# Input loads in equal halves, small loads moved, a value tile copied in place, recurrent states first on VectorE

## The chip, the cores and the metric

The kernel runs on one core of a Trainium2 chip. The metric is the time of one execution on the device in microseconds (us); the median of several runs is compared. The core has five engines that run side by side, each working through its own instructions in order: TensorE (PE in the profile; its weight loads are PEld), VectorE (DVE), ScalarE (ACT), GpSimd (POOL) and SyncE (SP), which here only issues DMA transfers. [...]

## The reference

One layer of a diffusion backbone on 640 tokens: 128 context tokens and 512 latent tokens, each a row of 1024 numbers. All in 32-bit floats.

```
shift, scale, gate = split(silu(c) @ w_ada + b_ada)
h    = rmsnorm(x, g_pre) * (1 + scale) + shift
proj = h @ w_in                                  # 3840 columns
a    = attention: 8 heads of 64; latent tokens see a window of the grid plus 256 cached context keys
r    = two gated linear recurrences (forward, backward), 4 heads, state 64 x 64 a head
f    = real part of a 2-D Fourier transform over positions and channels, then a 256 x 256 matrix
out  = concat(a * silu(ga), rmsnorm(r) * silu(gr), f * silu(gf)) @ w_out
y    = x + gate * rmsnorm(out, g_post)
```

Context and latent tokens have modulation vectors of their own. The latent recurrences start from given states; the context's final states, keys and values are outputs too.

## The kernel before

All products of weights with activations are done three times on TensorE, since each 32-bit operand is split into a high and a low part (hi, lo: a cast on ScalarE, line 130, and a subtraction on VectorE, line 131), and hi x hi, hi x lo and lo x hi are added up in PSUM. `mm` at line 113 issues every product, `tr` at line 127 every transpose through TensorE.

Start: `load_x` (line 217) reads the input in five tiles of 128 tokens. Each tile comes in two transfers, columns 0 to 639 into `xa` and 640 to 1023 into `xb`. `scale_x` sums the squares of `xa` on ScalarE (line 225) and of `xb` on VectorE (line 226), makes the reciprocal root and scales both halves on VectorE (lines 230, 231). `start_stream` then takes eight modulation steps k: two 512 KB blocks of the modulation weights (wss) are multiplied with the activated conditioning vector (`mod_cols`), the result is brought into columns, the scaled input's column block k is transposed (`xcols` picks it) and modulated into hT. The weights of the first three steps are loaded ahead. `zf_stream` multiplies the first projection blocks as the blocks of hT appear.

Small constants come first: cc (the conditioning vectors) and lbl (the logits of the recurrences' lower bound) on SP's queue, bss, gpre and sel on GpSimd's. sel is a 0/1 selector for the gate vectors; `gate_vectors` (line 853) copies it at line 855 and uses it late in the kernel. cc is needed for csil (line 171), lbl for a short chain on VectorE and ScalarE (lines 154 to 160).

Loads of weights go through `load_raw`, which chains each SP transfer behind the weight transfer issued before it (`wdma`, an order of issue, not a wait); `load` queues other transfers behind the last weight transfer so far.

The rest: a fixed list (FILL) says in which order projection blocks are traced: zb0, qr0, zb1, qr1, ir0 for the recurrences, then four pairs of attention heads P0 to P3 between gate and Fourier blocks. Generators for the two recurrences (`recurrence(p)`, two heads each), the attention and the gate vectors are woven in by a small planner (`Order`) with assumed latencies. The framework then orders the traced instructions of every engine: by its own model of their durations it takes the ready one of the highest priority, which is the order of tracing unless `tc.high_priority()` lifts a block of them. So an edit in one place can change the order elsewhere.

A recurrence runs seven levels over blocks of 1, 2, 4 ... 64 tokens: copies of the operands on ScalarE (lines 468 to 471), four multiplications on VectorE (474 to 477), products on TensorE and a masked copy into AL and AC on VectorE (458). Then come the states: for each of two directions four 128 x 128 products into a PSUM tile pst, the context's final state copied out (`fin`, line 519), and along the chunks state = state x decay + product (line 532, three chunks times two heads). The decays lie in small tiles of tag "m" (four buffers, shared with softmax scratch); pst and the level products share five PSUM buffers of tag "b".

For each pair of attention heads, `by_token` (line 345) transposes the value tile, five blocks, into PSUM; the fifth is copied by ScalarE into an "m" tile (line 354), and ScalarE and VectorE split the result into vs. Tiles of tag "t", the value tile among them, share 18 buffers.

Of the kernel before, what the change touches and what calls it, by code (L numbers as in the profile page):

```python
# [12 lines left out]
ACT = mybir.ActivationFunctionType  # L13
ALU = mybir.AluOpType
# [3 lines left out]
P = 128  # L18
D = 1024
KT = 8  # L20
NT = 640
# [50 lines left out]
def mixer_kernel(ctx: ExitStack, tc: tile.TileContext, A, O):  # L72
    nc = tc.nc
    sc, ve, gp, te, sy = nc.scalar, nc.vector, nc.gpsimd, nc.tensor, nc.sync
# [12 lines left out]
    def nm(s):  # L87
        n_[0] += 1
        return f"{s}_{n_[0]}"

    def T(cols=NT, dt=F32, tag=""):
        return tp.tile([P, NT], dt, tag="t", name=nm("t" + tag))[:, :cols]

    def PE_():
        return tp.tile([P, 512], F32, tag="pe", name=nm("pe"), bufs=WB["pe"])

    def S(cols):
        if cols <= 16:
            return sp.tile([P, 16], F32, tag="s", name=nm("s"))[:, :cols]
        return sp.tile([P, 320], F32, tag="m", name=nm("m"), bufs=WB["m"])[:, :cols]  # L100
# [4 lines left out]
    def PB(tag="b"):  # L105
        return ps.tile([P, 512], F32, tag=tag, name=nm("pb"), bufs=WB["p" + tag])
# [3 lines left out]
    def mm(out, lhsT, rhs, start=True, stop=True):  # L110
        n, m = rhs.free_size(), lhsT.free_size()
        od.now += 1e-3 * (n * 0.4167 * 4 if rhs.dtype == F32 else max(n * 0.4167, m * 0.83)) + 2e-3
        return te.matmul(out, lhsT, rhs, start=start, stop=stop).ins  # L113
# [11 lines left out]
    def tr(out, src):  # L125
        od.now += 0.107
        last_tr[0] = te.transpose(out, src, ident).ins  # L127

    def split(src, hi, lo, hi_eng=None, lo_eng=None):
        (sc.copy if hi_eng is None else hi_eng.tensor_copy)(hi, src)  # L130
        (ve if lo_eng is None else lo_eng).tensor_sub(lo, src, hi.bitcast(F32))  # L131
# [5 lines left out]
    def const(name, shape, dt=F32, dma=gp.dma_start):  # L137
        t = cp.tile([P, *shape], dt, tag=name, name=name)
        if name in A:
            dma(t, A[name])  # L140
        return t

    cc = const("cc", [KT, 2], dma=sy.dma_start)
    lbl = const("lbl", [2, 2], dma=sy.dma_start)
    bss = const("bss", [KT, 2])
    gpre = const("gpre", [KT])
    sel = const("sel", [2, P])
    RS = [slice(0, 64), slice(64, 128)]
    eps = cp.tile([P, 1], F32, tag="eps", name="eps")
    ve.memset(eps, EPS)  # L150
# [11 lines left out]
    def rsqrt_mean(ss, n):  # L162

        sc.activation(ss, ss, ACT.Sqrt, bias=eps, scale=1.0 / n)
        ve.reciprocal(ss, ss)
# [7 lines left out]
    wdma, nb = [], [1]  # L173

    def load_raw(src, tag, shape=(KT, P)):
        t = (tp if tag == "vs" else wp).tile([P, *shape], F32, tag=tag, name=nm(tag), bufs=WB[tag])
        with tc.issue_after(wdma[-1]) if wdma else ExitStack():
            wdma.append(sy.dma_start(t, src).ins)
        return t
# [10 lines left out]
    def load(t, src):  # L190

        with tc.issue_after(wdma[-1]) if wdma else ExitStack():
            sy.dma_start(t, src)

    def mod_cols(out, w, chain):

        t = od.now
        for k in range(KT):
            run_mm(chain, out[32 * (k % 4):32 * (k % 4) + 32, :], csil[:, k, :], w[:, k, :], start=(k < 4), stop=(k >= 4))
        od.now = t + 0.45  # L200

    shift, G, rstd = const("shift", [KT, 2]), const("G", [KT, 2]), const("rstd", [5])
    hT = [big.tile([P, KT, NT], F32R, tag=f"hT{j}", name=f"hT{j}") for j in range(2)]
    xa, xb = [T(tag="xa") for _ in range(5)], [T(384, tag="xb") for _ in range(5)]

    def xcols(i, k):
        return (xa[i] if k < 5 else xb[i])[:, k % 5 * P:k % 5 * P + P]
    zf_w, zf_acc = [], [[PB("f"), PB("f")], [PB("f"), PB()]]

    def mm3(out, w, k, u, first, last):  # L210
# [5 lines left out]

    def load_x():
        for i in range(5):
            load(xa[i], A["x"][i * P:(i + 1) * P, 0:NT])
            load(xb[i], A["x"][i * P:(i + 1) * P, NT:D])  # L220

    def scale_x():
        for i in range(5):
            ss2 = S(2)
            sc.activation(T(), xa[i], ACT.Square, accum_out=ss2[:, 0:1])
            ve.tensor_tensor_reduce(PE_()[:, 0:384], xb[i], xb[i], 1.0, 0.0, op0=ALU.mult, op1=ALU.add,
                                    accum_out=ss2[:, 1:2])
            ve.tensor_add(rstd[:, i:i + 1], ss2[:, 0:1], ss2[:, 1:2])
            rsqrt_mean(rstd[:, i:i + 1], D)
            ve.tensor_scalar(xa[i], xa[i], rstd[:, i:i + 1], 0.0, op0=ALU.mult, op1=ALU.add)  # L230
            ve.tensor_scalar(xb[i], xb[i], rstd[:, i:i + 1], 0.0, op0=ALU.mult, op1=ALU.add)
# [11 lines left out]

    def start_stream():
        load_x()
        raws, zraw = [], []

# [98 lines left out]
    def by_token(src, copy_last=False):  # L346

        pt = PB(), PB("f")
        for i in range(5):
            tr(pt[i // 4][:, i % 4 * P:i % 4 * P + P], src[:, i * P:(i + 1) * P])  # L350
        last = pt[1][:, 0:P]
        if copy_last:
            last = S(P)
            sc.copy(last, pt[1][:, 0:P])
        return [(slice(4 * j, 4 + j), (pt[0], last)[j].rearrange("p (i e) -> p i e", e=P)) for j in range(2)]

# [66 lines left out]
    def recurrence(p):  # L423
# [88 lines left out]
        for d in range(2):  # L512
            Td = (Tf, Tb)[d]
            pst = PB()
            for a, i in enumerate([0] + order[d][:3]):
                mm(pst[:, a * P:(a + 1) * P], kt[d][:, a * P:(a + 1) * P], vr[p][:, i, :])
            fin = sp.tile([P, 64], F32, tag="fin", name=nm("fin"), bufs=2)
            for hh in range(2):
                ve.tensor_copy(fin[RS[hh], :], pst[RS[hh], 64 * hh:64 * hh + 64])
            sy.dma_start(O["o_st"][d, p], fin)  # L520
            sall = T(512)
            gp.memset(sall, 0.0)
            for a, i in enumerate(order[d]):
                for hh in range(2):
                    r = RS[hh]
                    cdst = slice(a * P + 64 * hh, a * P + 64 * hh + 64)
                    if a == 0:
                        gp.tensor_copy(sall[r, cdst], late["st"][r, p, d, :])
                    else:
                        ip = order[d][a - 1]  # L530
                        cs = slice((a - 1) * P + 64 * hh, (a - 1) * P + 64 * hh + 64)
                        ve.scalar_tensor_tensor(sall[r, cdst], sall[r, cs], Td[r, ip:ip + 1], pst[r, cdst],  # L532
                                                op0=ALU.mult, op1=ALU.add)
                Sst[d][i] = sall[:, a * P:(a + 1) * P]
        yield LAT["st"]

# [314 lines left out]
    gg = [[None, None], [None, None]]  # L851

    def gate_vectors():
        selr = cp.tile([P, 2, P], F32R, tag="selr", name="selr")
        gp.tensor_copy(selr, sel)
        for q in range(8):
            yield f"block{WG + q}"
            hf = q // 4
            w = load_raw(A["wg"][q], "raw")
            if q % 4 == 0:  # L860
                gbias = T(512), T(512)
                for t, name in zip(gbias, ("bgate", "gpost")):
                    load(t, A[name][hf * 512:hf * 512 + 512].partition_broadcast(P))
                if True:
                    if q == 0:
                        gc = sp.tile([P, 2, 512], F32, tag="masks", name="gc", bufs=1)
                    gg[0][hf], gg[1][hf] = gc[:, hf, :], T(512)
                else:
                    gg[0][hf], gg[1][hf] = T(512), T(512)
            if q % 2 == 0:  # L870
                rows = [sp.tile([P, 256], F32R, tag="AC", name=nm("row"), bufs=2) for _ in range(2)]
            pm, es = PB("f"), slice(q % 2 * P, q % 2 * P + P)
            mod_cols(pm[:, 0:P], w, [])
            split(pm[:, 0:P], *[t[:, es] for t in rows])
            if q % 2 == 0:
                continue
            yield 1.0
            pg, cs = PB("f"), slice(q % 4 * P - P, q % 4 * P + P)
            for d in range(2):
                for a in range(2):  # L880
                    mm(pg[:, d * 256:d * 256 + 256], selr[:, d, :], rows[a], start=(a == 0), stop=(a == 1))
            for d in range(2):
                g = gg[d][hf][:, cs]
                ve.tensor_add(g, pg[:, d * 256:d * 256 + 256], gbias[0][:, cs])
                ve.tensor_mul(g, g, gbias[1][:, cs])
# [108 lines left out]

    od.add(late_consts())
    od.add(recurrence(0))
    od.add(recurrence(1))
    od.add(attentions())
    od.add(gate_vectors())
    od.add(fill())  # L1000
    od.run()
# [136 lines left out]
```

## Time and profile before

| | |
|---|---|
| median of 3 runs | 434.32 us (433.76 to 434.38) |
| the profiled execution | 434.13 us |
| its span | 432.3 us |
| TensorE busy | 409.4 us (95%) |
| VectorE busy | 303.0 us (70%) |
| ScalarE busy | 205.8 us (48%) |
| GpSimd busy | 7.4 us (2%) |
| moved by DMA | 47.62 MB, 110 GB/s over the span |

A line of the profile names the start and length in us (or a count, busy time and mean), the engine, the line of the kernel, the operation, output<-input, and the number of instructions as x16. In brackets stands how long the engine had been idle before it and what released it. SPq and POOLq are queues that issue transfers.

### The profile page before, as it was taken

The numbers are of one execution on the slowest core, as the hardware profiler recorded it, in microseconds if no ns is written. First come the engines' busy times: TensorE is split into PE (matmuls) and PEld (weight loads), VectorE is DVE, ScalarE is ACT, GpSimd is POOL, SyncE is SP. The second block draws the span as 40 slices with busy tenths as digits, with TensorE's granted clock in tenths as the row PEclk, the third lists the DMA queues.
The fourth block names the chain that finished last, engine by engine and source line by source line (L and its number), as shares of the span: only waits on it lengthen the run. The fifth ranks groups of instructions, "written<-read, shape, count | busy, mean of one in ns | idle before, by whom it ended". The sixth has DMA issues, their size and how long they took to land.

```text
span 432.3 us, 8308 instructions
## 1 busy us (share of the span) xinstructions
PE 409.4 (95%) x3176; PEld 372.6 (86%) x3176; DVE 303.0 (70%) x866; ACT 205.8 (48%) x551; POOL 7.4 (2%) x23
## 2 busy tenths in 40 slices
PE   0699999999998999999999999999999999999994
PEld 0488999999988998999899989899898889988884
DVE  3775579999896966885598657786679748471164
ACT  6525466566342526754445634744466553341331
POOL 2000000000020000000000000000000000000000
PEclk9999999999999999999999999999999999999998
DMA  7996154101202021122012522245323202245032
GB/s 236 414 407 237 49 176 141 61 16 50 99 12 75 9 62 49 56 98 74 33 60 72 143 73 90 90 154 159 105 101 122 89 9 102 85 156 198 0 147 99
DMA packets 19528, 47.62 MB, mean 110 GB/s; under 512 B 3184, under 2 KB 6912, under 8 KB 19488
## 3 DMA queue, kind: packets, MB, share of 16 engines
q1 hardware_dynamic: 19376, 46.94, 31.3%
q8 instruction: 25, 0.41, 0.4%
q0 software_dynamic: 112, 0.14, 0.3%
q14 instruction: 15, 0.12, 0.1%
HBM read 43.80 MB, written 3.28 MB: 109 GB/s over the span
## 4 chain that ended last, share of the span: by engine, by line
PE 90%; DVE 4%; DMA 3%; ACT 1%; issue 0%; SPq 0%; DVEq 0%
PE pb L113 84%; PE pb L127 7%; DMA vs<-wss 1%; DMA txa<-x 1%; DVE t L532 1%; DVE AL L458 1%; DVE AL L495 0%; ACT L688 0%; DVE lo L131 0%; DVE t L960 0%; ACT hi L130 0%; ACT pe L688 0%; ACT pe L689 0%; DVE t L475 0%; DVE t L474 0%
## 5 line engine op out<-in xcount | busy, mean ns | idle before, releaser
L113 PE MATMUL pb<-hT,hi 128*128 128x320 f32 x896 | 207.8, 316 | 0.5 <-DVE t L131 0.4
L113 PEld LDWEIGHTS pb<-hT,hi 128*128 128x128 f32 x896 | 149.5, 188 | 6.4 <-issue 1.1
L113 PE MATMUL pb<-hT,lo 128*128 128x320 f32 x448 | 139.7, 313 | 0.0
L113 PEld LDWEIGHTS pb<-hT,lo 128*128 128x128 f32 x448 | 84.1, 188 | 1.4 <-DVE G L274 0.2
L131 DVE TENSOR_TENSOR lo<-raw,hi 128x1024 fp32r<-128x1024 f32 x35 | 42.7, 1221 | 21.8 <-ACT hi L130 21.5
L130 ACT CAST hi<-raw 128x1024 fp32r<-128x1024 f32 x35 | 36.7, 1049 | 35.2 <-PE pb L113 19.5
L113 PE MATMUL pb<-t,t 64*128 64x128 f32 (+2 forms) x414 | 43.1, 291 | 1.9 <-DVE t L532 1.5
L113 PEld LDWEIGHTS pb<-t,t 64*128 64x128 f32 (+1 forms) x414 | 36.2, 188 | 6.3 <-issue 2.3
L113 PE MATMUL pb<-hi,mh 128*128 128x512 f32 (+1 forms) x108 | 32.1, 376 | 0.0
L130 ACT CAST pT<-pb 128x256 fp32r<-128x256 f32 x64 | 22.9, 371 | 16.3 <-DVE pT L131 9.8
L131 DVE TENSOR_TENSOR pT<-pb,pT 128x256 fp32r<-128x256 f32 x64 | 26.3, 416 | 1.6 <-ACT pT L130 1.3
L113 PEld LDWEIGHTS pb<-hi,mh 128*128 128x128 f32 x108 | 19.4, 189 | 3.2
L113 PE MATMUL pb<-pT,mh 128*128 128x512 f32 (+1 forms) x102 | 22.2, 364 | 0.0
L688 ACT ACTIVATE pe<-pb,s 128x256 f32<-128x256 f32 x32 | 15.2, 476 | 13.0 <-DVE s L687 7.7
L127 PE MATMUL pb<-ident,pe 128*128 128x128 f32 x136 | 20.8, 274 | 0.5 <-ACT pe L689 0.5
L943 ACT ACTIVATE t<-pb 128x512 f32<-128x512 f32 (+1 forms) x11 | 6.0, 551 | 30.5 <-PE pb L113 30.5
L113 PEld LDWEIGHTS pb<-pT,mh 128*128 128x128 f32 x102 | 17.7, 189 | 3.1
L113 PE MATMUL pb<-lo,mh 128*128 128x512 f32 (+1 forms) x54 | 20.2, 373 | 0.0
L127 PEld LDWEIGHTS pb<-ident,pe 128*128 128x128 f32 x136 | 16.5, 140 | 1.7 <-ACT pe L689 0.7
L458 DVE COPY_PREDICATED AL<-masks,pb 128x512 f32<-128x512 uint32 x24 | 16.5, 738 | 1.9 <-PE pb L113 1.8
L113 PE MATMUL pb<-pT,vs 128*128 128x256 f32 (+1 forms) x96 | 17.2, 321 | 0.0
L699 DVE TENSOR_TENSOR o<-pb,o 64x512 f32<-64x512 f32 (+1 forms) x16 | 7.8, 487 | 13.3 <-ACT o L698 13.2
(209 smaller groups left out, 630.1 us busy)
## 6 DMA issues: line engine op xcount, KB each, us to landing
raw<-win SPq DMA_DIRECT2D x30, 512.0 KB, 3.3
pT<-wss SPq DMA_DIRECT2D x12, 512.0 KB, 10.2
raw<-wg SPq DMA_DIRECT2D x8, 512.0 KB, 3.4
raw<-wout SPq DMA_DIRECT2D x8, 512.0 KB, 3.3
t<-x SPq DMA_DIRECT2D x10, 256.0 KB, 5.8
o_y<-t SPq DMA_DIRECT2D x9, 256.0 KB, 2.1
vs<-wss SPq DMA_DIRECT2D x4, 512.0 KB, 9.1
tbl<-tbl SPq DMA_DIRECT2D x4, 512.0 KB, 3.3
```

The lines of the kernel that those rows point to most:

```text
L113: return te.matmul(out, lhsT, rhs, start=start, stop=stop).ins
L127: last_tr[0] = te.transpose(out, src, ident).ins
L130: (sc.copy if hi_eng is None else hi_eng.tensor_copy)(hi, src)
L131: (ve if lo_eng is None else lo_eng).tensor_sub(lo, src, hi.bitcast(F32))
L458: ve.copy_predicated(out, mk.to_broadcast([P, i1 - i0, P]), src)
L532: ve.scalar_tensor_tensor(sall[r, cdst], sall[r, cs], Td[r, ip:ip + 1], pst[r, cdst], op0=ALU.mult, op1=ALU.add)
L688: sc.activation(pe[:, 256:512], ss[:, 256:512], ACT.Exp, bias=m[:, 1:2], accum_out=m[:, 3:4])
L699: ve.tensor_add(out, src[r, :], out)
L943: sc.activation(T(512)[:, cs], po[:, 0:cs.stop - cs.start], ACT.Square, accum_out=ssb[:, j:j + 1])
```

## The change

- `load_x` and `scale_x`: each tile is loaded as 512 + 512 columns; the ten loads enter the chain `wdma` of weight transfers. ScalarE squares 512 columns instead of 640, VectorE 512 instead of 384.
- lbl and cc are loaded through ScalarE's queue, lbl first.
- sel is no longer loaded at the start through GpSimd's queue but in `gate_vectors`, through `load`, on SP's queue.
- `by_token` with `copy_last` copies the fifth block over the fifth block of its source, in place of a tile of its own.
- In `recurrence`, the copies to `fin` and the state updates get high priority.

```diff
-    cc = const("cc", [KT, 2], dma=sy.dma_start)
-    lbl = const("lbl", [2, 2], dma=sy.dma_start)
+    lbl = const("lbl", [2, 2], dma=sc.dma_start)
+    cc = const("cc", [KT, 2], dma=sc.dma_start)
     bss = const("bss", [KT, 2])
     gpre = const("gpre", [KT])
-    sel = const("sel", [2, P])
...
-    xa, xb = [T(tag="xa") for _ in range(5)], [T(384, tag="xb") for _ in range(5)]
+    xa, xb = [T(512, tag="xa") for _ in range(5)], [T(512, tag="xb") for _ in range(5)]
     def xcols(i, k):
-        return (xa[i] if k < 5 else xb[i])[:, k % 5 * P:k % 5 * P + P]
+        return (xa[i] if k < 4 else xb[i])[:, k % 4 * P:k % 4 * P + P]
...
     def load_x():
         for i in range(5):
-            load(xa[i], A["x"][i * P:(i + 1) * P, 0:NT])
-            load(xb[i], A["x"][i * P:(i + 1) * P, NT:D])
+            for u, t in enumerate((xa[i], xb[i])):
+                with tc.issue_after(wdma[-1]) if wdma else ExitStack():
+                    wdma.append(sy.dma_start(t, A["x"][i * P:(i + 1) * P, 512 * u:512 * u + 512]).ins)
     def scale_x():
...
-            sc.activation(T(), xa[i], ACT.Square, accum_out=ss2[:, 0:1])
-            ve.tensor_tensor_reduce(PE_()[:, 0:384], xb[i], xb[i], 1.0, 0.0, op0=ALU.mult, op1=ALU.add,
+            sc.activation(T(512), xa[i], ACT.Square, accum_out=ss2[:, 0:1])
+            ve.tensor_tensor_reduce(PE_(), xb[i], xb[i], 1.0, 0.0, op0=ALU.mult, op1=ALU.add,
                                     accum_out=ss2[:, 1:2])
...
         if copy_last:
-            last = S(P)
+            last = src[:, 4 * P:5 * P]
             sc.copy(last, pt[1][:, 0:P])
...
-            for hh in range(2):
-                ve.tensor_copy(fin[RS[hh], :], pst[RS[hh], 64 * hh:64 * hh + 64])
+            with tc.high_priority():
+                for hh in range(2):
+                    ve.tensor_copy(fin[RS[hh], :], pst[RS[hh], 64 * hh:64 * hh + 64])
...
-                        ve.scalar_tensor_tensor(sall[r, cdst], sall[r, cs], Td[r, ip:ip + 1], pst[r, cdst],
-                                                op0=ALU.mult, op1=ALU.add)
+                        with tc.high_priority():
+                            ve.scalar_tensor_tensor(sall[r, cdst], sall[r, cs], Td[r, ip:ip + 1], pst[r, cdst],
+                                                    op0=ALU.mult, op1=ALU.add)
...
     def gate_vectors():
+        sel = const("sel", [2, P], dma=load)
         selr = cp.tile([P, 2, P], F32R, tag="selr", name="selr")
         gp.tensor_copy(selr, sel)
```

## The prediction

> **What bounds the kernel now.** I read the page first, then who TensorE waited for, then two stretches in order of time.
>
> ```profile
> span 432.3 us, 8308 instructions
> PE 409.4 (95%) x3176; PEld 372.6 (86%) x3176; DVE 303.0 (70%) x866; ACT 205.8 (48%) x551; POOL 7.4 (2%) x23
> ```
>
> ```profile
> PE pb L113 <- DMA vs<-wss: 14.0, 1, 14.0
> PE pb L113 <- DVE t L532: 1.5, 1, 1.5
> PE pb L127 <- ACT pe L689: 0.5, 1, 0.5
> PE pb L113 <- DVE t L131: 0.4, 1, 0.4
> PE pb L113 <- DVE AL L458: 0.4, 1, 0.4
> ```
>
> ```profile
> 0.00:14.00 14.00, 0.04 (x4) 0.07 (x6) 6.52 (x30) 9.25 (x19) 3.08 (x11) 1.00 0.84 278
> 119.00:133.00 14.00, 12.10 (x110) 10.64 (x107) 13.09 (x39) 5.07 (x14) 2.42 (x6) 1.00 0.04 9
> 133.00:160.00 27.00, 27.00 (x225) 26.31 (x225) 20.16 (x53) 10.86 (x29) 1.91 (x6) 1.00 0.19 58
> ```
>
> The page says TensorE bound, 95%. The change touches none of its matmuls, so it can only win where TensorE stands still. The list of waits names all those places: 14.0 us before the first weights of the modulation (wss) land, 1.5 us once for the state instruction L532 of the recurrence, and three waits of half a microsecond or less. In the table of stretches (after the length: busy TensorE, weight loads, VectorE, ScalarE, GpSimd, clock, share of DMA, GB/s) the start is a DMA stage (0.84 busy). From 119 to 133 VectorE is busy 13.09 of 14.00 us and TensorE only 12.10. In the next 27 us TensorE is full, and the list has no long wait after it, so time won in either place should reach the end.
>
> **The start.** What changes: two small loads leave SP's queue, the selector's load (sel) leaves the front, and the input comes as 512 + 512 columns in place of 640 + 384.
>
> ```profile
> 0.73 0.39 SPq L140 DMA_DIRECT2D cc<-cc  x1
> 1.18 0.42 SPq L140 DMA_DIRECT2D lbl<-lbl  x1
> 1.65 0.42 SPq L193 DMA_DIRECT2D txa<-x  x1
> 7.49 0.74 ACT L225 ACTIVATE t<-txa 128x640 f32<-128x640 f32 x1 [1.43 <-DMA txa<-x]
> 9.87 0.56 DVE L226 CUSTOM_DVE_ANT_0 pe<-txb 128x384 f32<-128x384 f32 x1 [1.03 <-DMA txb<-x]
> 14.34 0.55 DVE L230 TENSOR_SCALAR txa<-txa,rstd 128x640 f32<-128x640 f32 x1
> 14.97 0.50 PEld L127 LDWEIGHTS pb<-ident,txa 128*128 128x128 f32 x3 [0.38 <-DVE txa L230]
> ```
>
> ```profile
> 6.00:8.00 2.00, 0.00 (x0) 0.00 (x0) 0.30 (x2) 0.57 (x2) 0.40 (x1) 1.00 1.01 287
> 10.00:12.00 2.00, 0.00 (x0) 0.00 (x0) 1.96 (x10) 1.83 (x6) 0.00 (x0) 1.00 1.07 420
> ```
>
> ```profile
> sel<-sel POOLq DMA_DIRECT2D x1, 128.0 KB, 4.4
> ```
>
> - Queue: SP issues the first input load at 1.65; with cc and lbl gone it can go at 0.73, 0.92 us sooner. The DMA engines are full from then on (share 1.01 and above), so the whole train of input and weights moves by that much.
> - sel: 128 KB out of that train at the 287 GB/s of its stretch is 0.45 us for all that lands behind it. Together the first weights land 0.92 + 0.45 = 1.37 us sooner.
> - VectorE: the sum of squares of the second half grows from 384 to 512 columns. Its own row has one width only, so I take the slope of other two-operand rows of VectorE shown below, 0.83 us for 640 columns and 0.49 for 320: 0.34 / 320 x 128 = 0.14 us a tile. VectorE has waits ahead of the first three tiles (the 1.03 us above is the last of them) and runs without a break afterwards, so three tiles pay: 0.41 us. The two scalings trade 128 columns and their sum stays. TensorE's first transposes wait for exactly this work (0.38 us at 14.97, for L230), so what gets through is not 1.37 but 1.37 - 0.41 = 0.96 us. ScalarE's Square becomes shorter by the same columns.
> - ScalarE issues cc and lbl ahead of its first table load, some 0.8 us by SP's rows. This costs nothing: lbl lands half a microsecond sooner than before, and ScalarE stood idle 1.43 us ahead of the second Square. Were that cover gone, it would cost the 0.8.
> - sel again: SP issues it behind the weights of modulation step 3, one issue and 128 KB, 0.31 us at 420 GB/s, ahead of the weights of steps 4 to 7. Their cover is in these rows:
>
> ```profile
> pT<-wss SPq DMA_DIRECT2D x12, 512.0 KB, 10.2
> 24.04 2.39 SPq L178 DMA_DIRECT2D pT<-wss  x3
> 41.71 1.08 PE L113 MATMUL pb<-pT,csil 128*32 128x128 f32 x32
> ```
>
> The last of them is issued by 26.43, lands some 10.2 us later, at about 36.6, and is used at 41.71: 5 us of cover for 0.31. sel's only reader (selr on GpSimd) is needed far later by the gate vectors.
>
> I take 0.9 us for the start; its bounds are 0 (all given back on VectorE or in issue order) and 1.4.
>
> **The states.** Rows of VectorE, TensorE and ScalarE, then groups of the stretch from 119 to 134:
>
> ```profile
> 125.78 0.48 DVE L477 TENSOR_TENSOR t<-t,m 128x320 f32<-128x320 f32 x1
> 126.38 0.45 DVE L519 COPY fin<-pb 64x64 f32<-64x64 f32 x2
> 127.48 0.49 DVE L474 TENSOR_TENSOR t<-t,m 128x320 f32<-128x320 f32 x1
> 132.11 1.22 DVE L532 SCALAR_TENSOR_TENSOR t<-t,m,pb 64x64 f32<-64x64 f32 x4
> 50.38 0.83 DVE L241 TENSOR_TENSOR hT<-t,hT 128x640 fp32r<-128x640 f32 x1
> ```
>
> ```profile
> 124.63 1.16 PE L113 MATMUL pb<-t,t 128*128 128x128 f32 x8 [0.36 <-DVE AL L458]
> 127.59 0.49 PE L113 MATMUL pb<-t,t 64*128 64x128 f32 x2
> 131.00 0.31 PE L113 MATMUL pb<-hT,lo 128*128 128x320 f32 x1
> 132.84 0.46 PE L113 MATMUL pb<-t,t 64*128 64x128 f32 x2 [1.53 <-DVE t L532]
> 126.29 0.46 ACT L471 COPY t<-t 128x320 f32<-128x320 f32 x1 [0.23 <-DVE t L477]
> 132.79 0.27 ACT L354 COPY m<-pb 128x128 f32<-128x128 f32 x1 [6.03 <-DVE t L532]
> ```
>
> ```profile
> L532 DVE SCALAR_TENSOR_TENSOR t<-t,m,pb 64x64 f32<-64x64 f32 x12 | 3.4, 280 | 0.4
> L519 DVE COPY fin<-pb 64x64 f32<-64x64 f32 x4 | 0.9, 219 | 0.1
> L113 PE MATMUL pb<-hT,hi 128*128 128x320 f32 x20 | 5.0, 329 | 0.0
> L113 PE MATMUL pb<-hT,lo 128*128 128x320 f32 x9 | 2.8, 308 | 0.0
> ```
>
> TensorE's state products of recurrence 0 are issued by 125.8. VectorE then needs 12 + 4 small instructions, 3.4 + 0.9 = 4.3 us, but spreads them from 126.38 to 133.33, since instructions of recurrence 1's levels (L474 at 127.48 is one) stand between. The level products at 132.84 read nothing of the states. They wait because PSUM buffers of tag "b" (five) are still held by the products that L532 reads. With priority the block runs from about 125.8 to 130.1, before TensorE runs dry at 131.31 (131.00 + 0.31), and the 1.53 us go. The instructions pushed aside are late by up to 4.3 us; the 29 projection matmuls of the stretch cover that, if the planner leaves them ahead of the level products.
>
> The copied value tile takes away ScalarE's 6.03 us wait: the tile of tag "m" that L354 wrote was held by the decays which L532 reads. The copy then runs at about 126.8, and the casts of the next weights behind it move up as well. TensorE waited for none of these, so I cost it at nothing; without it the 1.53 us might only have passed to the casts. In exchange the value tile, of tag "t" (18 buffers), lives until its splits have read it. Whoever waits for that buffer is ScalarE or VectorE, and hardly longer than the 6.03 us that the copy itself waited so far, a wait that TensorE's other work covered; I cost it at nothing too.
>
> I take 1.5 us; bounds are the loss worked out below and 1.53 + 0.36 = 1.9.
>
> **The sum.** The profiled run took 434.13 us, 1.8 us around its span of 432.3, and lies 0.19 under the median of 434.32. 434.13 - 0.9 - 1.5 = 431.73, on the median 431.9 us.
>
> **Rivals.**
> 1. The start is given back. TensorE ends its first steps at half its later rate:
>
> ```profile
> 22.57 1.02 PE L113 MATMUL pb<-vs,csil 128*32 128x128 f32 x16
> 26.96 1.08 PE L113 MATMUL pb<-pT,csil 128*32 128x128 f32 x32
> ```
>
> 16 products took 1.02 us at 22.57, and 32 took 1.08 at 26.96. If full rate begins at the same moment although TensorE starts 0.9 us sooner, the time won is filled at half rate and 0.45 remains; the sum is then 434.32 - 0.45 - 1.5 = 432.4. If VectorE or the new order eats all, 432.8. For it: VectorE is full from 9.87 on. Against it: the transposes depend on what moved. [...]
> 2. The wait at 132.84 takes another form. TensorE meets the next unfinished level there and stands about as long; only the start counts, 434.32 - 0.9 = 433.4. For it: VectorE is busy 13.09 of 14 us, and its sum of work is the same. Against it: the wait is for a buffer, not for work.
> 3. Slower: the state block runs over the operands of the next level. L477 at 125.78 feeds ScalarE's copy L471 and that the level products at 127.59. Behind 4.3 us of states L477 starts at 130.1, L471 ends at 131.0, and products placed at 127.59 are 3.4 us late. If TensorE's order leaves them where they are, it pays 3.4 - 1.5 = 1.9 us net, less 0.9 from the start: 435.3. It turns to a loss where fewer than 8 projection matmuls are put in front: 3.4 less the 2.4 of the forecast is 1.0 us, at 27.00 us / 225 = 0.12 us an instruction. The planner orders TensorE with VectorE's delay in view, and 29 such matmuls stand in the stretch, which speaks against it.
> 4. All of it comes through: start 1.4, states 1.9, and a little more where the scratch tile freed in "m" shortens the softmax waits (the 0.5 us for L689): 434.32 - 3.8 = 430.5.
>
> **Chances.** Forecast 0.46, rival 1 0.17, rival 2 0.14, rival 3 0.13, rival 4 0.10. 0.2% is about what a measurement of this kernel can tell, 0.87 us: faster is under 433.45, slower over 435.19. Forecast, rivals 1 and 4 are faster, 0.73; rival 2 lies on the edge, and I give it to "same", with a little of rival 1 for an order of the planner that comes out worse elsewhere: faster 0.71, same 0.16, slower 0.13. The range reaches from rival 4 with a little more, 430.2, over rival 2 to 434.5; above it is rival 3. The forecast's own range is 431.2 to 432.6.
>
> **What would show it.** Right: the first input load at about 0.7 and the first modulation products at about 12.6; transposes some 0.9 us sooner; the 16 state instructions in one block of some 4.5 us; no wait of TensorE for L532; L354 within a microsecond of its transpose. Wrong: a TensorE wait for L458 or L471 near 130; VectorE still scaling when the second modulation product has landed more than a microsecond before; new waits after 160, which would be the planner's order and not a part of the change.

## The result, and the profile after

The changed kernel takes 429.76 us (median of 4 runs, 429.45 to 430.12) beside 434.04 us for the kernel before (4 runs, 433.70 to 434.38): ratio 0.9902, 95% interval 0.9885 to 0.9919. That is 4.28 us less where 2.4 were forecast, and 0.44 us below the range. The profiled execution took 430.12 us beside 434.13.

The line of busy times and the list of TensorE's waits (line, who was waited for, total, times, longest), after the change:

```profile
PE 409.1 (96%) x3176; PEld 372.2 (87%) x3176; DVE 305.0 (71%) x866; ACT 205.3 (48%) x551; POOL 7.0 (2%) x22
```

```profile
PE pb L113 <- DMA vs<-wss: 12.2, 1, 12.2
PE pb L113 <- DVE AL L458: 0.4, 1, 0.4
PE pb L113 <- ACT t L237: 0.3, 1, 0.3
PE pb L127 <- DVE row L266: 0.3, 1, 0.3
```

The wait for the first weights is 1.8 us shorter. Three waits are gone: 1.5 us for the states (L532), 0.5 us for the probabilities (L689) and 0.4 us for L131. Two small ones at the start are new. In the table of stretches TensorE is now full from 133 to 345 (before, it was busy 184.08 of the 185.00 us from 160 on), and from 119 to 133 it gained what the state wait had cost:

```profile
119.00:133.00 14.00, 13.63 (x115) 12.33 (x114) 13.43 (x42) 6.37 (x17) 2.42 (x6) 1.00 0.05 11
133.00:160.00 27.00, 27.00 (x225) 26.20 (x225) 18.92 (x49) 9.81 (x26) 1.92 (x6) 1.00 0.19 58
160.00:345.00 185.00, 185.00 (x1411) 170.05 (x1410) 140.43 (x461) 101.81 (x323) 0.00 (x0) 1.00 0.29 92
```

Where the time came off is read from products that stand in both timelines. First before, then after:

```profile
124.63 1.16 PE L113 MATMUL pb<-t,t 128*128 128x128 f32 x8 [0.36 <-DVE AL L458]
157.76 0.98 PE L113 MATMUL pb<-kc,tqs 64*128 64x256 f32 x12
426.07 0.28 PE L113 MATMUL pb<-lo,mh 128*128 128x256 f32 x1
```

```profile
123.69 1.16 PE L113 MATMUL pb<-t,t 128*128 128x128 f32 x8 [0.37 <-DVE AL L458]
155.26 0.98 PE L113 MATMUL pb<-kc,tqs 64*128 64x256 f32 x12
422.14 0.28 PE L113 MATMUL pb<-lo,mh 128*128 128x256 f32 x1
```

The lead is 0.94 us ahead of the states, 2.50 behind them and 3.93 at the end: 0.94 from the start, 1.56 in the stretch of the state wait, 1.43 later, where the prediction had nothing. The two later waits account for 0.92 of that 1.43: between the second and the third of these products TensorE was busy 267.39 of 268.31 us before, and all of 266.88 after. The other 0.51 is shorter busy time of TensorE in the new order, and is not assigned to any part.

The start after the change:

```profile
0.73 0.39 SPq L220 DMA_DIRECT2D txa<-x  x1
3.91 0.33 SPq L220 DMA_DIRECT2D txa<-x  x1
3.91 0.16 DVE L153 TENSOR_TENSOR lb<-lbl 128x4 f32<-128x4 f32 x1 [3.05 <-DMA lbl<-lbl]
6.09 0.61 ACT L225 ACTIVATE t<-txa 128x512 f32<-128x512 f32 x1
9.88 0.16 DVE L164 RECIPROCAL rstd<-rstd 128x1 f32<-128x1 f32 x1 [0.70 <-ACT rstd L163]
12.24 1.08 PE L113 MATMUL pb<-vs,csil 128*32 128x128 f32 x16 [12.24 <-DMA vs<-wss]
15.73 0.42 DVE L266 COPY row<-pb 128x256 f32<-128x256 f32 x1
16.20 0.69 PE L127 MATMUL pb<-ident,row 128*128 128x128 f32 x2 [0.25 <-DVE row L266]
```

The first input load goes at 0.73, as foreseen. But lbl lands near 3.9 and not sooner than before, ScalarE's first Square is at 6.09, and SP's seventh input load stands until 3.91, where the rhythm of the earlier ones (0.47 us apart) would have put it at 3.54. VectorE waits 0.70 us for the first root that ScalarE makes (L163), and from 9.88 on it runs without a gap. It copies the first rows at 15.73, directly behind its scalings, and TensorE waits 0.25 us for that. Before, the copy was at 16.96, and it had waited 0.75 us for TensorE.

The states after the change, VectorE first, then ScalarE, then TensorE:

```profile
125.92 0.59 DVE L534 SCALAR_TENSOR_TENSOR t<-t,m,pb 64x64 f32<-64x64 f32 x2
126.54 0.49 DVE L474 TENSOR_TENSOR t<-t,m 128x320 f32<-128x320 f32 x1
133.03 0.29 DVE L534 SCALAR_TENSOR_TENSOR t<-t,m,pb 64x64 f32<-64x64 f32 x1
125.02 0.26 ACT L354 COPY t<-pb 128x128 f32<-128x128 f32 x1
130.21 0.46 PE L113 MATMUL pb<-hT,hi 128*128 128x320 f32 x2
132.71 0.31 PE L113 MATMUL pb<-hT,lo 128*128 128x320 f32 x1
132.94 0.49 PE L113 MATMUL pb<-t,t 64*128 64x128 f32 x2
```

There is no block: state instructions (now L534) still alternate with the levels of the other recurrence, and the last comes at 133.03. What is new is that ScalarE copies the value tile at 125.02 without a wait, and that eighteen more projection products (130.21 to 132.71) stand ahead of the level products at 132.94: behind the 16 products that start at 127.84 there are 26, and in the kernel before there were 8. (The expectation for the doubled states, further down, counts twelve.) In the kernel before, the others came behind the wait:

```profile
133.23 0.57 PE L113 MATMUL pb<-hT,hi 128*128 128x320 f32 x2
133.38 1.05 ACT L130 CAST hi<-raw 128x1024 fp32r<-128x1024 f32 x1
```

Their operands were there already: the next cast, which began only at 133.38, belongs to a later block. So TensorE had work that it could have done during its 1.53 us, but its order had put that work behind the wait.

### The profile page after: what moved, and what is told of

It reads as the page before. It is cut to its first block, busy times and chain, and to the rows that moved or that the text cites. A ratio compares the mean times of both kernels' runs of the same rounds, so it can differ in the third digit from the quotient of the medians.

```text
span 428.3 us, 8304 instructions
## 1 busy us (share of the span) xinstructions
PE 409.1 (96%) x3176; PEld 372.2 (87%) x3176; DVE 305.0 (71%) x866; ACT 205.3 (48%) x551; POOL 7.0 (2%) x22
## 4 chain that ended last, share of the span: by engine, by line
PE 91%; DVE 4%; ACT 2%; DMA 1%; issue 1%; SPq 0%; DVEq 0%; ACTq 0%
PE pb L113 85%; PE pb L127 6%; DMA txa<-x 1%; ACT t L237 1%; DVE txb L231 1%; DVE AL L458 0%; SPq L220 0%; DVE AL L495 0%; DVE hT L240 0%; ACT L283 0%; ACT L163 0%; DVE txa L230 0%; DVE lo L131 0%; DVE t L963 0%; ACT t L239 0%
## 5 line engine op out<-in xcount | busy, mean ns | idle before, releaser
L131 DVE TENSOR_TENSOR lo<-raw,hi 128x1024 fp32r<-128x1024 f32 x35 | 42.8, 1223 | 22.7 <-ACT hi L130 22.3
L113 PE MATMUL pb<-hi,mh 128*128 128x512 f32 (+1 forms) x108 | 30.6, 375 | 0.0
L131 DVE TENSOR_TENSOR pT<-pb,pT 128x256 fp32r<-128x256 f32 x64 | 26.6, 417 | 3.7 <-ACT pT L130 3.4
L113 PE MATMUL pb<-lo,mh 128*128 128x512 f32 (+1 forms) x54 | 19.3, 375 | 0.0
L458 DVE COPY_PREDICATED AL<-masks,pb 128x512 f32<-128x512 uint32 x24 | 16.7, 743 | 1.9 <-PE pb L113 1.8
```

The costliest lines, as they stand in the source:

```text
L458: ve.copy_predicated(out, mk.to_broadcast([P, i1 - i0, P]), src)
```

## The experiments

The change has three separable parts: the start (halves, small loads, sel), the copy of the value tile, and the priority. Each was run alone.

**The start alone.**

```diff
 all edits of load_x, scale_x, xcols, cc, lbl and sel as in the change;
 by_token and recurrence as in the kernel before
```

> The kernel before with the three edits of the start alone: equal halves, lbl and cc through ScalarE's queue, sel later. Theory: the start is worth what the traces show between 50 and 118 us, where the changed kernel's products run 0.95 us ahead; the waits for L532 (1.5 us), for L689 (0.5) and for the low part L131 (0.4) stay, so about 433.1 us, 0.95 less than before. Rival: the earlier start also moves the later stretches out of their waits (another order of instructions after 160 us), then 431.5 or less and the waits are gone.

Measured: 432.89 us (432.06 to 433.76, 12 runs) beside 433.86 of the kernel before (23 runs); ratio 0.9977, interval 0.9964 to 0.9990. So 0.97 us, the 0.9 of the prediction, and the state wait stays. Its profile shows one thing more. The wait, and then three stretches of 3 us (after the length: TensorE, weight loads, VectorE, ScalarE, GpSimd, granted clock, DMA share, GB/s):

```profile
131.27 0.46 PE L113 MATMUL pb<-t,t 64*128 64x128 f32 x2 [1.52 <-DVE t L532]
```

```profile
129.00:132.00 3.00, 1.48 (x10) 1.13 (x9) 2.78 (x9) 0.75 (x4) 0.00 (x0) 1.00 0.00 0
132.00:135.00 3.00, 3.00 (x14) 3.00 (x13) 3.00 (x8) 0.85 (x1) 0.00 (x0) 0.53 0.03 8
135.00:138.00 3.00, 3.00 (x26) 3.00 (x24) 0.00 (x0) 0.00 (x0) 0.00 (x0) 0.90 0.65 187
```

After 1.52 us of standing still the granted clock is 0.53, then 0.90. By these two numbers 0.47 x 3 + 0.10 x 3 = 1.7 us of clock are lost, an estimated 3.4 us at half rate. In the profile of the kernel before the same wait has no such stretch (clock 1.00 from 133 to 160).

**The copy alone.**

```diff
         if copy_last:
-            last = S(P)
+            last = src[:, 4 * P:5 * P]
```

> The kernel before with one line changed: the fifth block of the value tile is copied over its source. Theory now: this line alone removes the wait for L532, because the planner then puts more projection products ahead of the level products, and the later waits too; the changed kernel gains 1.55 us between 130 and 150 and about 1.5 more after 160, so about 431.0 us, 3.1 less than before. Rival, the prediction as made: the copy takes nothing off TensorE's path and is worth 0: 434.0 us.

Measured: 429.92 us (429.75 to 431.11, 6 runs) beside 433.86; ratio 0.9917, interval 0.9898 to 0.9937. The part that the prediction costed at nothing is worth 3.6 us by the ratio (2.7 to 4.4 by the interval; the medians differ by 3.94). With the start's 0.97 that is 4.6, the whole gain of 4.28 within these intervals. All three waits (L532, L689, L131) are gone:

```profile
PE pb L113 <- DMA vs<-wss: 13.6, 1, 13.6
PE pb L113 <- DVE hT L240: 0.5, 1, 0.5
PE pb L113 <- DVE AL L458: 0.4, 1, 0.4
```

**The priority alone.**

```diff
+            with tc.high_priority():
                 for hh in range(2):
                     ve.tensor_copy(fin[RS[hh], :], pst[RS[hh], 64 * hh:64 * hh + 64])
...
+                        with tc.high_priority():
                             ve.scalar_tensor_tensor(sall[r, cdst], sall[r, cs], Td[r, ip:ip + 1], pst[r, cdst],
                                                     op0=ALU.mult, op1=ALU.add)
```

> The kernel before with the priority of the state instructions alone. The prediction as made: 1.5 us less, 432.5 us, with the sixteen instructions in one block. Theory now: the instructions of all five engines stand in the same order as before, so nothing changes: 434.0 us, and the wait of 1.5 us for the state instruction is still there.

Measured: 434.02 us (432.60 to 435.68, 12 runs) beside 433.86; ratio 1.0003, interval 0.9985 to 1.0021. All five engines have their instructions in the same order as in the kernel before, and the waits are the same:

```profile
PE pb L113 <- DVE t L534: 1.5, 1, 1.5
PE pb L127 <- ACT pe L691: 0.5, 1, 0.5
PE pb L113 <- DVE t L131: 0.4, 1, 0.4
```

So the priority does nothing here.

**The value tile into a buffer of another tag.** This tells "copied over its source" from "no longer takes a tile of tag m".

```diff
-            last = S(P)
+            last = sp.tile([P, P], F32, tag="pc", name=nm("last"), bufs=2)
```

> The kernel before, with the fifth block copied into another small tile (tag pc, not in use until 200 us) in place of one of tag m; nothing is copied over its source. If the cause is the buffer of tag m that the copy waited for, the copy runs within a microsecond of its transpose and the 1.5 us at the level products go: 432.5 us or less, with what the other order of instructions gives after 160 us. If it is the copying over the source as such (another life of the value tile), it stays at 434.0 us.

Measured: 430.09 us (429.44 to 431.29, 6 runs) beside 433.86; ratio 0.9917, interval 0.9897 to 0.9938. Its waits:

```profile
PE pb L113 <- DMA vs<-wss: 13.9, 1, 13.9
PE pb L113 <- DVE AL L458: 0.4, 1, 0.4
```

Nothing is copied in place here, and the gain is the same. What counts is the "m" tile that the copy no longer takes.

**The whole change without the priority.**

> The whole change without the priority for the states; what is issued on each of the five engines stands in the same order as with it. Theory of the prediction's second step: the priority is what takes the 1.5 us wait at 132.84 away, so the time goes back to 431.3 or more (429.76 + 1.5). Theory now: the priority changes nothing and the copy of the value tile is what took the wait away, so the time is that of the whole change, 429.8 give or take 0.4, ratio 0.990, with no wait for line 534 and no stretch at half clock after 130 us.

Measured: 429.63 us (429.25 to 430.20, 4 runs) beside 433.16; ratio 0.9916, interval 0.9901 to 0.9930. The time of the whole change, as the second theory had it.

**Another order with the "m" tile still taken.** Each reordering could lose two small waits by chance, so the kernel before was given another order for the work after 150 us.

```diff
-        "prep": 5.0, "sm": 4.0, "pT": 1.6, "mx": 2.0}
+        "prep": 7.0, "sm": 4.0, "pT": 1.6, "mx": 2.0}
```

> The kernel before with one due time of its planner changed and nothing else: TensorE's order is the same up to about its instruction 1020 (some 150 us) and differs in 69 places after that; the value tile still takes a scratch buffer. In the kernel before TensorE waits 1.5 us for the states at 132.84, 0.5 us for the probabilities (line 689) near 172 and 0.4 us for a scratch product (line 131) near 340; the copy alone lost all three. Theory 1, the scratch buffer that the value tile held was behind the two later waits: they or their like stay in this kernel, and the time is 434 (ratio 0.999 to 1.001). Theory 2, the two later waits hang on the order in which the planner happens to put things: one or both are gone here too, though the buffer is still held, and the time is some 0.5 to 1 us less (ratio 0.9975 to 0.999). The wait for the states stays in both.

Measured: 433.73 us (432.85 to 436.31, 12 runs) beside 434.42 (17 runs); ratio 0.9993, interval 0.9976 to 1.0009. Waits among others:

```profile
PE pb L113 <- DVE t L532: 1.5, 1, 1.5
PE pb L113 <- DVE s L666: 1.4, 1, 1.4
PE pb L127 <- ACT pe L689: 0.5, 1, 0.5
```

The wait for L689 stays; the one near 340 us is now for a softmax instruction (L666, before L131) and grows to 1.4. One other order is not proof, but it gives no support to chance: with the buffer held, waits of this kind stay.

**The start, edit by edit.** One profile each: only the halves, only cc and lbl through ScalarE, only sel later (432.68, 434.40 and 433.45 us; single runs, from which nothing is read of the time).

> Only the cut of the input tiles into two halves of 512 columns, everything else as before. In the kernel before, the first modulation weights land at 13.83 us and the first products start at 13.96; with the whole change they land at 12.1 and start at 12.24, which is 0.35 us more than the 1.37 that the prediction had worked out from the slots of the two small loads (0.92) and the 128 KB less ahead of the weights (0.45). Theory of the prediction: equal halves move the same bytes in the same ten loads, so first products at 13.96 give or take 0.15. Rival: the halves are where the missing 0.35 comes from, so 13.6 or sooner. The wait of 1.5 us for the states and the 6 us wait for the value tile stay in both.

> Only the two smallest loads (cc and lbl) moved from SyncE's queue to ScalarE's. Theory of the prediction: the first input load is issued 0.92 us sooner and all that follows on that queue with it, so first products at 13.04 (13.96 - 0.92). Rival, from the profile of the changed kernel, where the label landed at 3.9 us instead of 2.9 and SyncE's seventh input load stood behind it: a part of the 0.92 is given back in the queue, so first products between 13.2 and 13.6, and the first Square of the input near 6.1 instead of 5.23.

> Only the load of the selector (sel, 128 KB with its rows) moved behind the weights, to the place where the gates are worked out. Theory of the prediction: 0.45 us less ahead of the first weights, so first products at 13.5 (13.96 - 0.45). Rival: the weights wait for their turn in the queue and not for bytes, so 13.9 to 14.0. A second rival: 0.8 or more, which would put the missing 0.35 us here.

The first modulation products, in this order (13.96 before, 12.24 with the whole change):

```profile
13.56 1.08 PE L113 MATMUL pb<-vs,csil 128*32 128x128 f32 x16 [13.56 <-DMA vs<-wss]
```

```profile
12.91 1.08 PE L113 MATMUL pb<-vs,csil 128*32 128x128 f32 x16 [12.91 <-DMA vs<-wss]
```

```profile
13.16 1.08 PE L113 MATMUL pb<-vs,csil 128*32 128x128 f32 x16 [13.16 <-DMA vs<-wss]
```

0.40, 1.05 and 0.80 us sooner, 2.25 in all, where the three together gave 1.72. But each is one execution, and this moment moves by itself: over the profiles of the kernels whose start is the old one, TensorE's wait for the first weights is 13.6 to 14.1 us (13.6 in that of the copy alone), and 12.2 to 13.1 over those with the whole new start. So the 0.40 of the halves can't be told from nothing, as forecast. cc and lbl are near their 0.92, and that sel is worth more than its 0.45 is likely but not shown. Where the missing 0.35 came from stays open, and it is within what one execution differs from another.

The price of the small loads, as the prediction did not see it, in the list of transfers (KB, then us from issue to landing), with cc and lbl through ScalarE and then before:

```profile
lbl<-lbl ACTq DMA_DIRECT2D x1, 2.0 KB, 3.4
```

```profile
lbl<-lbl SPq DMA_DIRECT2D x1, 2.0 KB, 1.7
```

With cc and lbl through ScalarE's queue the load of 2 KB takes 3.1 to 3.4 us in six profiles; ahead of the input on SP's queue it takes 1.6 or 1.7 in six others. But in the profile with only sel moved it is issued on SP's queue ahead of the input, as before, and takes

```profile
lbl<-lbl SPq DMA_DIRECT2D x1, 2.0 KB, 2.9
```

So the queue alone does not account for the late landing, and its cause stays open.

**The states twice.** The whole change without the priority, and each state product issued two times with the same result.

```diff
-                        ve.scalar_tensor_tensor(sall[r, cdst], sall[r, cs], Td[r, ip:ip + 1], pst[r, cdst],
-                                                op0=ALU.mult, op1=ALU.add)
+                        for _ in range(2):
+                            ve.scalar_tensor_tensor(sall[r, cdst], sall[r, cs], Td[r, ip:ip + 1], pst[r, cdst],
+                                                    op0=ALU.mult, op1=ALU.add)
```

> The kernel of e5_no_states with every state product on VectorE (12 for each pair of heads, about 0.29 us each) issued twice in a row; the second writes the same value, so nothing is left out and 24 instructions are added. The order of TensorE's instructions is the same up to its instruction 858 (about 131 us) and differs by 58 after that. In the changed kernel 12 more projection products stand ahead of the state products than before and TensorE does not wait for the states. Theory 1, that cover is short: the states come some 2 us later for the first pair, TensorE waits 1 us or more for line 534 or its like near 133, some runs show the stretch at half clock behind it, and the time is 431 to 433. Theory 2, the order has cover to spare: no wait over 0.4 us, no half clock after 130 us, and the time is within 0.4 us of e5_no_states.

Measured: 439.09 us (437.65 to 439.47, 4 runs), 9.5 us over the same kernel without the doubling, for 24 instructions of about 0.29 us, 7.0 us of VectorE. That is well past what either theory had. Its waits, the longest of them in the timeline, and the stretches behind it:

```profile
PE pb L113 <- DVE t L533: 4.3, 2, 3.0
```

```profile
137.90 0.68 PE L113 MATMUL pb<-t,t 128*128 128x128 f32 x4 [3.03 <-DVE t L533]
```

```profile
139.00:142.00 3.00, 3.00 (x22) 2.78 (x22) 1.12 (x2) 0.27 (x1) 0.00 (x0) 0.52 0.00 0
142.00:145.00 3.00, 3.00 (x26) 2.81 (x25) 0.50 (x3) 0.67 (x2) 1.17 (x3) 0.92 0.00 0
```

3.5 us more of VectorE for the first pair came back as a wait of 3.0 us, and the clock fell to half behind it (0.48 x 3 + 0.08 x 3 = 1.7 us lost). The second pair paid again with the rest of the 4.3 us, another wait (L508) took 0.9, and the mean clock of the four runs is 0.986 to 0.992. How much cover the order of the changed kernel has is not shown by this: the doubled kernel got an order of its own from about 131 us on. It still has its level products at 133.23 without a wait, and the 3.03 us come at later products.

**An attempt to go further.** After 10.56 us VectorE is without a gap at the start, so three scalings were moved to ScalarE.

```diff
-            ve.tensor_scalar(xb[i], xb[i], rstd[:, i:i + 1], 0.0, op0=ALU.mult, op1=ALU.add)
+            if i >= 2:
+                sc.activation(xb[i], xb[i], ACT.Identity, scale=rstd[:, i:i + 1])
+            else:
+                ve.tensor_scalar(xb[i], xb[i], rstd[:, i:i + 1], 0.0, op0=ALU.mult, op1=ALU.add)
```

> The kernel of e5_no_states with the scaling of the second halves of tokens 2 to 4 moved from VectorE to ScalarE, which is idle from 12.06 to 13.99 there. After the change VectorE is busy without a gap from 10.56 to 17.19 us, and TensorE's products are 1.72 us sooner than before at first and 1.24 sooner from 16 us on. Theory 1, VectorE sets the start: three scalings of 0.40 us less (0.40 is their spacing, 15.33 to 15.73) bring the row copies up to 1.2 us sooner, of which TensorE's own work (3.94 us from 12.24 to the end of the two rows at 16.89 has 0.25 of waits) can give back some 0.25 to 0.5, so 429.2 to 429.5. Theory 2, TensorE's rate before its clock rises sets the start: 0.25 us at most, 429.5 to 429.8, the same as e5_no_states within 0.2%.

Measured: 430.01 us (429.45 to 430.36, 4 runs) beside 433.16; ratio 0.9922, interval 0.9907 to 0.9937. In its profile the row copy comes at 15.56 and now waits for TensorE:

```profile
15.56 0.42 DVE L269 COPY row<-pb 128x256 f32<-128x256 f32 x1 [0.47 <-PE pb L113]
```

1.2 us less on VectorE brought the copy 0.17 us ahead of 15.73, and nothing in the time. What the copy waits for there is TensorE, still at its lower rate (16 products in 1.08 us from 14.41, in 0.65 from 20.82). That its clock rises there, as the second theory has it, is not shown: the granted clock is 1.00 in every microsecond from 12 to 25 in the profiles before and after, and only the lengths of the products tell the rate.

## Why the prediction was right or wrong

**The start: the sum held.** 0.9 forecast, 0.97 measured alone and 0.94 in the profile. Within it the weights came 1.72 us sooner in this profile, not 0.92 + 0.45 = 1.37; since that moment differs by half a microsecond and more between executions, no term of the two is shown to be wrong. VectorE then took back 0.49 at the row copy (1.72 - 1.23) where 0.41 had been worked out, and 0.3 more was gone by 45 us, with a wait of TensorE of 0.27 (L237) among it. That 0.49 and 0.41 are close is at least in part luck. Three tiles were to pay for longer sums in the stretch without a gap; but that stretch starts at 9.88, no sooner than before (9.87), and holds two of the sums where it held three. What VectorE lost was its 0.75 us to spare at the row copy. Wrong outright is "lbl lands half a microsecond sooner", by a microsecond and a half: its chain starts at 3.91, and 2.93 before. Nor is it shown that this cost nothing: ScalarE's Squares start at 6.09 instead of 5.23 and stand ahead of the first root, for which VectorE waits 0.70 us before its stretch.

**The states: right about the 1.5 us, wrong about the cause.** The step that failed is "with priority the block runs from about 125.8 to 130.1". The priority moved no instruction. The wait went because the copy of the value tile changed TensorE's order, which put eighteen ready products ahead of the level products. That the 1.56 comes so close to the 1.5 is luck: the wait that was counted went, but not by the step that was to remove it.

**The copy, "I cost it at nothing": this step failed too, and made the number wrong.** The prediction saw ScalarE's wait of 6.03 us for the held "m" tile, and argued that TensorE waited for none of what stands behind it. In the timeline that is true. But the order of the instructions is made beforehand, with the same buffer held in it, and that order is what TensorE paid for: 1.56 us at the states and 1.43 later. With the tile freed, the waits for L689 (172 us) and L131 (340 us) are gone too; of the kernels above, those with the buffer held have such waits after 150 us and those with it freed have none, except the doubled states, with waits of their own. Just how the framework comes to the other order was not tried, and stays open.

**A term that was missing: the clock behind a wait.** The prediction charged the wait with its length. In some executions it costs more. Seven profiles have the wait of 1.5 us. In the three of them with a mean clock of 0.992 or 0.993 (the start alone, only cc and lbl, the other planner order) the clock falls behind the wait, to 0.53 and 0.90, 0.66 and 0.77, 0.57 and 0.86 in two stretches of 3 us: 1.7 us lost each time. In the other four, at 0.996 or 0.997, it does not. Of the 47 further runs of the kernel before that go with the experiments, 18 have a mean granted clock of 0.994 or less (8 of 23, 10 of 17 and none of 7, by group) and a median of 434.53 us; the other 29 have a median of 433.39. In all 24 runs of kernels without the wait (the whole change with and without the priority, the copy alone, the other tag, the scalings) the clock is 0.995 or more. So the wait cost 1.1 us more in about four of ten of these executions, an estimated 0.4 us in the mean, and that left with it.

**The sum.** 0.9 + 1.5 = 2.4 forecast. Profile against profile it was 0.94 + 1.56 + 1.43 = 3.93, and by the medians 4.28; the clock behind the wait is an estimated 0.4 on top, in the mean. Rival 4 had the place of the later gain right (the scratch tile in "m", the wait for L689) with a chance of 0.10 and some 0.5 us for it; its other half, more at the start and at the states, did not come.

**The other rivals.** Rival 1 had the half rate at the start as a fixed moment. It is not fixed, and no run shows what sets it: the kernel with the priority alone has the same instructions in the same order as the kernel before, and yet TensorE reaches full rate sooner. The 16 products of 22.57 (1.02 us, quoted in the prediction; 0.64 is their length at full rate) take there

```profile
22.24 0.64 PE L113 MATMUL pb<-vs,csil 128*32 128x128 f32 x16
```

and the wait for L458, at 124.63 before, comes at 123.91, 0.72 us sooner with nothing changed:

```profile
123.91 1.16 PE L113 MATMUL pb<-t,t 128*128 128x128 f32 x8 [0.37 <-DVE AL L458]
```

So a single profile can't tell 0.7 us at the start from chance, and that the forecast 0.94 agrees so well with the profile is partly luck; the timed 0.97 (0.4 to 1.6 by its interval) is the better witness. Rival 2 (another wait in its place) did not come; in the doubled states something like it did, at a load and in an order of their own. Rival 3 needed the block, which never formed.

## What to carry to other kernels

A long wait of an engine off the critical path can name a buffer that is held too long. Before it is costed at nothing, ask not only who waits for that engine now, but what order was made around it: giving the copy either of two other buffers was worth 3.6 us here. And an edit of priorities is worth nothing until the order of the instructions is seen to differ.

## What the hardware showed that was not expected

Behind a wait of 1.5 us TensorE's granted clock fell to 0.53 to 0.66 in one stretch of 3 us and was 0.77 to 0.90 in the next (an estimated 3.4 us at half rate), in three of the seven profiles that have the wait; in the other four it stayed at 1.00. The mean clock is 0.994 or less in 18 of 47 further executions of the kernel before, which has this wait. Behind the wait of 3.0 us in the doubled states the clock was 0.52, then 0.92. What decides whether the clock falls is not shown by these runs.

The moment of full rate at the start moved by an estimated microsecond or more between two executions of the same instruction order (16 products in 1.02 us from 22.57 in one, in 0.64 from 22.24 in the other), and what follows moved by 0.7 us (the products behind the wait for L458 from 124.63 to 123.91, those behind the wait for the states from 132.84 to 132.10).

A queue of its own did not bring a load of 2 KB in sooner: beside the input's loads it landed after 3.1 to 3.4 us, instead of 1.6 or 1.7 ahead of them on their queue (2.9 in one profile).
